# One transfer over 128 partitions in place of two over 64 for each query and key tile of an attention

## The chip, the cores and the metric

The kernel runs on one core of a Trainium2 chip. The metric is the device time of one execution in microseconds, the median of several runs. TensorE (PE) multiplies matrices; VectorE (DVE), ScalarE (ACT) and GpSimd (POOL) work on elements; SyncE (SP) issues most of the transfers between the chip's memory (DRAM) and the on-chip memory (SBUF), which has 128 partitions. ACT and POOL issue some transfers too. 16 DMA engines carry them out.

## The reference

One layer of a decoder trunk over 1024 tokens of width 1024, in float32. Its parts: an input norm and one combined projection; attention over eight heads of 64; an RWKV-7 time mixing; an output projection with a norm and a residual; and a feed-forward block of width 4096. The change touches the attention alone:

```python
h = _rms_norm(x, norm_mix_pre[i])
z = h @ (w_in_first if i == 0 else w_in_rest[i - 1])
q = z[..., 0:D_ATTN]
k = z[..., D_ATTN:2 * D_ATTN]
v = z[..., 2 * D_ATTN:3 * D_ATTN]
...
s = jnp.einsum('bdhnqc,bdhnkc->bdhnqk', qblk, kb) * (1.0 / math.sqrt(Dh))
s = jnp.where(valid, s, -jnp.inf)
p = jnp.exp(s - m[..., None])
acc = jnp.einsum('bdhnqk,bdhnkc->bdhnqc', p, vb)
```

Three branches with different windows and strides are computed and combined by their denominators; the kernel does all three at once, by adding a mask (the "strip") that holds minus the logarithm of how many branches admit a pair of query and key.

## The kernel before

A float32 product is split in the kernel: each operand is a high part, rounded to a shorter type (fp32r), and a low part, the rest. The projection writes the high and the low part of q and k to a DRAM buffer `qk_d` (eight blocks of 128 rows, two parts, 1024 columns; a block holds a pair of heads, 64 rows for each). The high parts are written by ACT's queue (L724), the low ones by POOL's (L725).

The attention goes over four pairs of heads. For a pair p, `at_load` (L881) makes six tiles of 128 partitions by 1024, three for each of its two heads. `qs` has the high part of the head's queries in partitions 0 to 63 and the low part in 64 to 127. `kh` has the high part of the head's keys in both halves, `kl` the low part in both. So a product of `qs` with `kh`, and one with `kl` added to it, give the full scores over a contraction of 128. Each half of each tile is one transfer (L889), issued by SP: 12 for a pair, 48 in all, each 64 rows of 4 KB. The strip is loaded after the first head of pair 0.

The tiles lie in two sets; pairs 0 and 2 use one, pairs 1 and 3 the other, so a load of pair 2 or 3 waits until TensorE is done with the tiles of two pairs before. The set of pairs 1 and 3 lies in memory that comes free when the projection ends, in the course of pair 0.

64 steps, numbered m, go over the pairs, the groups of 128 queries (in the order 0, 4, 1, 5, 2, 6, 3, 7) and the two heads. A step computes the scores (`at_s`, tile `pS`, product by TensorE, mask and row minimum by DVE, exponential by ACT) two steps ahead of the transposes (`at_t`, tile `pT`) and the product with the values (`at_v`, tile `po`). Within pair 0 the second and the third step are exchanged: its first head has two groups before the second head has one. TensorE's order is that of the program text (a manual schedule) and TensorE goes through it strictly; the rest of the last projection (`z_av`) and later the first products of the output projection (`pm`) stand between the steps. The orders of the other engines are made by a scheduler from priorities; each engine then goes through its own strictly too. So does SP: an issue that waits holds back all issues behind it.

`at_load(0)` comes ahead of the steps, `at_load(1)` at m = 8, `at_load(2)` at m = 17 and `at_load(3)` at m = 33. Among SP's issues between them are the values of a pair (`vT`, L896), the output projection's weights (`wo`, L977), inputs for the residual (`xr`, L1047), results of the time mixing (`mr`, L1017) and the attention's output (`a_d`, L966).

The transfers of SP and ACT report their landing on eight counters taken in turn (DMAHW0 to DMAHW7 in the rows below), those of POOL on others (DMASW). A transfer waits until the one before it on its own counter has landed, hence the eighth before it in the program.

Of the kernel before, what the change touches and what calls it, by code (L numbers as in the profile page):

```python
# [10 lines left out]
F32 = mybir.dt.float32  # L11
# [8 lines left out]
P = 128  # L20
S = 1024
# [21 lines left out]
def hybrid_kernel(tc, x, par, cst, strip, win, wup_lora, gup, gnwb, grow, wout, wup, wdown, out, dbg=None):  # L43
    nc = tc.nc
# [21 lines left out]
    with (  # L66
# [60 lines left out]
        qk_d = dp.tile([8, 2, P, S], F32, name="qk_d")  # L127
# [252 lines left out]
        own = (slice(0, 64), slice(64, 128))  # L380
# [452 lines left out]
        st, HVs, VUs, Ys, Ns, N2, VZ, KR, IN, ZP = {}, {}, {}, {}, {}, {}, {}, {}, {}, {}  # L833
# [47 lines left out]
        def at_load(p):  # L881

            T = {(nm, h): aset[p % 2][h].tile([P, S], F32R, name=f"{nm}{p}_{h}", tag=f"{nm}{h}", bufs=1) for h in (1, 0) for nm in ("qs", "kh", "kl")}
            at[p] = QS, KH, KL = [[T[nm, h] for h in range(2)] for nm in ("qs", "kh", "kl")]
            for h in range(2):
                hs_ = slice(64 * h, 64 * h + 64)
                for L, q, js in ((QS, p, (0, 1)), (KH, 4 + p, (0, 0)), (KL, 4 + p, (1, 1))):
                    for d in range(2):
                        nc.sync.dma_start(L[h][own[d]].bitcast(F32), qk_d[q, js[d], hs_, :])  # L889
                if (p, h) == (0, 0):  # L890
                    nc.sync.dma_start(stripT, strip)

# [250 lines left out]
        with hi_pri():  # L1143
            at_load(0)
            at_raw(0)
            at_s(*step(0))
            at_s(*step(1))
        for m in range(64):
            p, h = m // 16, m % 2
            i = m % 16 // 2  # L1150
            with hi_pri():
                if m + 2 < 64:
                    at_s(*step(m + 2))
                at_t(*step(m))
                if h == 1 and i % 2 == 0 and m > 1:
                    at_v(*((p, i - 2) if i else (p - 1, 6)))
                if h == 1 and i == 0:
                    at_vt(p)
                    if p < 3:
                        at_raw(p + 1)  # L1160
                if m == 17 or m == 33:
                    at_load(p + 1)
            if m < RST:
                next(rest, None)
            if m == RST:
                for _ in rest:
                    pass
                open_mix()
                with hi_pri():
                    at_load(1)  # L1170
# [253 lines left out]
        with tc.tile_pool(name="ffd", bufs=1) as fp:  # L1424
            gpF = fp.tile([P, D], F32, name="gpF")
            E1, E2, E3 = ([fp.tile([P, 512], F32, name=f"E{k}_{q}") for q in range(4)] for k in (1, 2, 3))
            st = fp.tile([P, 8, 8], F32, name="stF")
# [202 lines left out]
```

## Time and profile before

| what | value |
|---|---|
| median of 3 runs | 1301.14 us (1300.73 to 1302.78) |
| the profiled execution | 1298.4 us |
| its span, first to last instruction | 1296.6 us |
| memory traffic | 241.08 MB, mean 186 GB/s |
| mean granted TensorE clock | 0.997 |

A row of the lines view gives line, engine, operation, written and read tiles, and count. A row of a timeline gives the start and length in us; in square brackets stand the idle time of the engine before the row and what ended it. "SPq" is SP's issuing of transfers. A row of the list of issues ends in the size of one transfer and the median us from issue to landing. A window row gives the busy time of PE, its weight loads, DVE, ACT and POOL with counts, and then the granted clock of PE, the mean busy share of the 16 DMA engines, and GB/s.

### The profile page before, as it was taken

How to read it: one execution, taken by the hardware profiler on the slowest of the kernel's cores; microseconds unless marked ns; L12 is line 12 of the kernel's file. 1: busy time of each engine (PE TensorE's matmuls, PEld its weight loads, DVE VectorE, ACT ScalarE, POOL GpSimd, SP SyncE). 2: the span in 40 equal slices, each digit the busy share in tenths (PEclk: the TensorE clock that was granted, in tenths of full speed). 3: DMA queues.
4: the chain of work that ended last, by engine and by line, in shares of the span. 5: the costliest groups of instructions: out<-in, count | busy, mean ns of one | idle time of the engine just before them, and what ended most of it. 6: DMA issues, size and time to landing. Idle time of an engine off the chain costs nothing.

```text
span 1296.6 us, 23887 instructions
## 1 busy us (share of the span) xinstructions
PE 1257.5 (97%) x9488; PEld 1035.1 (80%) x9488; DVE 902.8 (70%) x1647; ACT 623.7 (48%) x1052; POOL 43.2 (3%) x61
## 2 busy tenths in 40 slices
PE   6999999999999899999999999999999999999997
PEld 5778888877777678888887888888888888888886
DVE  7877679443868567567879976676666866446884
ACT  8653433233554387666656443444443544443442
POOL 0000000000000000000000000000000002000221
PEclk9999999999999999999999999999999999999999
DMA  6456767976795787314424644444567984556642
GB/s 243 144 191 162 206 159 198 276 219 217 210 264 167 234 238 196 99 56 139 149 96 141 218 142 160 163 146 144 173 210 240 380 296 139 178 189 198 193 160 105
DMA packets 168255, 241.08 MB, mean 186 GB/s; under 512 B 56688, under 2 KB 93808, under 8 KB 168144
## 3 DMA queue, kind: packets, MB, share of 16 engines
q1 hardware_dynamic: 158640, 213.86, 52.8%
q10 hardware_dynamic: 8064, 20.98, 4.8%
q0 software_dynamic: 1440, 4.72, 1.0%
q8 instruction: 75, 1.23, 0.4%
q14 instruction: 36, 0.29, 0.1%
HBM read 162.16 MB, written 77.09 MB: 185 GB/s over the span
## 4 chain that ended last, share of the span: by engine, by line
PE 80%; DVE 7%; DMA 6%; ACT 4%; issue 2%; SPq 1%; ACTq 0%; DVEq 0%
PE dX L49 12%; PE X L49 12%; PE pm L49 7%; PE dZ L49 7%; PE Z L49 6%; PE z_v L49 3%; PE dY L49 3%; PE z_aq L49 3%; PE Y L49 3%; PE z_r L49 3%; PE z_ak L49 2%; PE z_k L49 2%; PE pS L49 2%; PE z_av L49 2%; PE po L49 2%; PE pT L939 2%
## 5 line engine op out<-in xcount | busy, mean ns | idle before, releaser
L49 PE MATMUL dX<-wow,wou 128*128 128x512 f32 x768 | 175.1, 389 | 0.3 <-DVE wow L1247 0.3
L49 PEld LDWEIGHTS dX<-wow,wou 128*128 128x128 f32 x768 | 144.0, 188 | 30.7 <-DVE wow L1247 0.9
L49 PE MATMUL dZ<-wow,wou 128*128 128x512 f32 x384 | 87.4, 389 | 0.0
L49 PEld LDWEIGHTS dZ<-wow,wou 128*128 128x128 f32 x384 | 72.1, 188 | 15.0
L1247 DVE TENSOR_TENSOR wou<-ur,wou 128x1024 fp32r<-128x1024 f32 x56 | 71.2, 1273 | 6.5 <-ACT wou L1246 6.4
L1246 ACT ACTIVATE wow<-wd 128x1024 fp32r<-128x1024 f32 x32 | 33.8, 1060 | 70.6 <-PE dX L49 24.5
L1246 ACT ACTIVATE wou<-ur 128x1024 fp32r<-128x1024 f32 x56 | 58.5, 1048 | 15.6 <-DMA ur<-u_d 8.3
L1247 DVE TENSOR_TENSOR wow<-TK,wow 128x1024 fp32r<-128x1024 f32 x24 | 30.6, 1274 | 50.0 <-ACT wow L1246 50.0
L1247 DVE TENSOR_TENSOR wow<-wd,wow 128x1024 fp32r<-128x1024 f32 x32 | 39.5, 1236 | 29.5 <-ACT wow L1246 29.3
L927 DVE CUSTOM_DVE_ANT_0 S<-pS,stripT 128x512 f32<-128x512 f32 (+3 forms) x64 | 37.7, 589 | 26.3 <-PE pS L49 23.6
L1344 ACT ACTIVATE r<-u 128x512 f32<-128x512 f32 x48 | 30.1, 626 | 53.5 <-DVE u L1342 53.5
L1246 ACT ACTIVATE wow<-TK 128x1024 fp32r<-128x1024 f32 x24 | 25.4, 1059 | 63.0 <-PE dX L49 32.5
L929 ACT ACTIVATE S<-S,mn 128x128 f32<-128x128 f32 (+7 forms) x64 | 49.3, 771 | 11.1 <-DVE mn L927 10.8
L49 PE MATMUL pm<-WO,mxr 128*128 128x512 f32 x192 | 49.1, 400 | 0.8 <-DVE mxr L1012 0.8
L1552 POOL TENSOR_TENSOR E<-E,gpF 128x512 f32<-128x512 f32 x12 | 22.4, 1881 | 781.5 <-DMA xf<-x_d 621.3
L939 PE MATMUL pT<-cst,S 128*128 128x128 f32 x288 | 44.0, 278 | 4.0 <-ACT PT L941 1.7
L49 PE MATMUL z_av<-hT,wh_av 128*128 128x512 f32 x128 | 46.0, 411 | 1.9 <-DVE evl_ak L723 1.9
L49 PE MATMUL pm<-WO,mxa 128*128 128x512 f32 x192 | 46.1, 395 | 0.2 <-ACT mxa L1011 0.2
L49 PE MATMUL Z<-HB,wo 128*128 128x512 f32 x192 | 46.1, 389 | 0.0
L49 PE MATMUL z_aq<-hT,wh_aq 128*128 128x512 f32 x128 | 44.2, 404 | 0.0
L49 PE MATMUL dY<-wow,wou 128*128 128x512 f32 x192 | 43.7, 389 | 0.0
L49 PE MATMUL z_ak<-hT,wh_ak 128*128 128x512 f32 x128 | 43.7, 402 | 0.0
(396 smaller groups left out, 3066.5 us busy)
## 6 DMA issues: line engine op xcount, KB each, us to landing
ur<-u_d SPq DMA_DIRECT2D x56, 512.0 KB, 4.4
u_d<-S SPq DMA_DIRECT2D x64, 256.0 KB, 2.1
wd<-in_wdown_dram SPq DMA_DIRECT2D x32, 512.0 KB, 4.4
u_d<-u SPq DMA_DIRECT2D x48, 256.0 KB, 2.3
TK<-in_wdown_dram SPq DMA_DIRECT2D x24, 512.0 KB, 6.2
wr_upa<-in_wup_dram SPq DMA_DIRECT2D x16, 512.0 KB, 3.5
wr_upb<-in_wup_dram SPq DMA_DIRECT2D x16, 512.0 KB, 4.1
x<-in_x_dram SPq DMA_DIRECT2D x8, 512.0 KB, 7.1
```

The lines of the kernel that those rows point to most:

```text
L49: return PE.matmul(o, lhsT, rhs, start=start, stop=stop, skip_group_check=True)
L927: V.tensor_tensor_reduce(Sx[:, lo:hi], pS[:, :hi - lo], stripT[:, so:so + hi - lo], 1.0, 3e38 if k == 0 else mn[:, 0:1], OP.add, OP.min, a ...
L929: A.activation(Sx[:, :w], Sx[:, :w], AF.Exp, scale=-1.0, bias=mn[:, nbk - 1:nbk], accum_out=at[p, "den"][:, i, h:h + 1])
L939: PE.transpose(pt[:, j], Sx[:, (4 * k + j) * P:(4 * k + j + 1) * P], ident)
L1246: A.activation(w[:, 0, 0:n], raw, AF.Copy)
L1247: low = E.tensor_tensor(w[:, 1, 0:n], raw, w[:, 0, 0:n].bitcast(F32), OP.subtract)
L1344: A.activation(r, src, AF.Relu)
L1552: G.tensor_tensor(e, e, gn[n], OP.mult)
```

## The change

```diff
-                for L, q, js in ((QS, p, (0, 1)), (KH, 4 + p, (0, 0)), (KL, 4 + p, (1, 1))):
-                    for d in range(2):
-                        nc.sync.dma_start(L[h][own[d]].bitcast(F32), qk_d[q, js[d], hs_, :])
+                for L, q, j, st in ((QS, p, 0, P * S), (KH, 4 + p, 0, 0), (KL, 4 + p, 1, 0)):
+                    v = qk_d[q, j, hs_, :]
+                    nc.sync.dma_start(L[h].bitcast(F32), bass.AP(tensor=v.tensor, offset=v.offset, ap=[[st, 2], [S, 64], [1, S]]))
```

A tile is now filled by one transfer. Its source is an access pattern written by hand, a list of steps and counts from the outermost to the innermost. Before, both sides of a transfer were 64 rows of 1024 elements: [[1024, 64], [1, 1024]]. Now the destination is [[1024, 128], [1, 1024]], and the source [[131072, 2], [1024, 64], [1, 1024]] for `qs` (the step from the high part to the low part) and [[0, 2], [1024, 64], [1, 1024]] for `kh` and `kl` (the same 64 rows twice). The program as built carries these patterns unchanged.

SP's order at the load of pair 0, before (`qs_0` is the tile of head 0, `qs_1` of head 1, and `x2` stands for two equal rows):

```order
L889 DMA qs_0_5309<-qk_d 64x1024 x2
L889 DMA kh_0_5310<-qk_d 64x1024 x2
L889 DMA kl_0_5311<-qk_d 64x1024 x2
L891 DMA stripT<-in_strip_dram 128x1024
L889 DMA qs_1_5306<-qk_d 64x1024 x2
L889 DMA kh_1_5307<-qk_d 64x1024 x2
L889 DMA kl_1_5308<-qk_d 64x1024 x2
L896 DMA vT_5325<-zs_d 128x1024
```

and with the change:

```order
L889 DMA qs_0_5309<-qk_d 128x1x1024
L889 DMA kh_0_5310<-qk_d 128x1x1024
L889 DMA kl_0_5311<-qk_d 128x1x1024
L891 DMA stripT<-in_strip_dram 128x1024
L889 DMA qs_1_5306<-qk_d 128x1x1024
L889 DMA kh_1_5307<-qk_d 128x1x1024
L889 DMA kl_1_5308<-qk_d 128x1x1024
L896 DMA vT_5319<-zs_d 128x1024
```

The order is the same, with one issue where two stood.

SP's order from the values of pair 1 over the load of pair 1, before, with what each issue waits for (PE_49 and the like are progress counters of engines):

```order
L896 DMA vT_5395<-zs_d 128x1024 [waits DMAHW6_49,DMAHW3_49,PE_49]
L977 DMA wo_6970<-in_wout_dram 128x1024 [waits DMAHW7_49,DMAHW4_49,DVE_49]
L889 DMA qs_0_5565<-qk_d 64x1024 [waits DMAHW5_49,PE_49]
L889 DMA qs_0_5565<-qk_d 64x1024 [waits DMASW4_49]
L889 DMA kh_0_5566<-qk_d 64x1024 [waits DMAHW0_49]
L889 DMA kh_0_5566<-qk_d 64x1024 [waits DMAHW1_49]
L889 DMA kl_0_5567<-qk_d 64x1024 [waits DMAHW2_49,DMASW7_49,DMASW6_49]
L889 DMA kl_0_5567<-qk_d 64x1024 [waits DMAHW3_49]
L889 DMA qs_1_5562<-qk_d 64x1024 [waits DMAHW4_49]
```

and with the change, up to the first issue of pair 2's load:

```order
L896 DMA vT_5389<-zs_d 128x1024 [waits DMAHW6_49,PE_49]
L889 DMA qs_0_5559<-qk_d 128x1x1024 [waits DMAHW7_49,DMASW4_49,PE_49]
L889 DMA kh_0_5560<-qk_d 128x1x1024 [waits DMAHW1_49]
L889 DMA kl_0_5561<-qk_d 128x1x1024 [waits DMAHW2_49,DMASW7_49,DMASW6_49]
L889 DMA qs_1_5556<-qk_d 128x1x1024 [waits DMAHW3_49]
L889 DMA kh_1_5557<-qk_d 128x1x1024 [waits DMAHW4_49]
L889 DMA kl_1_5558<-qk_d 128x1x1024 [waits DMAHW5_49]
L977 DMA wo_7017<-in_wout_dram 128x1024 [waits DMAHW6_49,DVE_49]
L1047 DMA xr_7462<-in_x_dram 128x1024 [waits DMAHW7_49,DVE_49]
L1047 DMA xr_7535<-in_x_dram 128x1024 [waits DMAHW0_49,DVE_49]
L889 DMA kh_0_5884<-qk_d 128x1x1024 [waits DMAHW1_49,PE_49]
```

The load of pair 1 still follows the `vT` of pair 1 and still waits for PE. Three `wo` and `xr` issues now stand between the loads of pairs 1 and 2; one `wo` issue moved ahead of `vT`. Where before two issues made up a tile, the counters are passed at half the pace, so a wait on a counter reaches back over more tiles.

SP's order at the load of pair 3, before:

```order
L977 DMA wo_7041<-in_wout_dram 128x1024 [waits DMAHW1_49,Activation_49]
L1047 DMA xr_7486<-in_x_dram 128x1024 [waits DMAHW2_49,Activation_49]
L1047 DMA xr_7559<-in_x_dram 128x1024 [waits DMAHW3_49,Activation_49]
L889 DMA qs_0_6384<-qk_d 64x1024 [waits DMAHW4_49,PE_49]
L889 DMA qs_0_6384<-qk_d 64x1024 [waits DMAHW5_49,DMASW6_49,DMASW4_49]
L889 DMA kh_0_6385<-qk_d 64x1024 [waits DMAHW6_49]
L889 DMA kh_0_6385<-qk_d 64x1024 [waits DMAHW7_49]
L889 DMA kl_0_6386<-qk_d 64x1024 [waits DMAHW0_49,DMASW7_49,DMASW1_49]
```

and with the change:

```order
L1047 DMA xr_7634<-in_x_dram 128x1024 [waits DMAHW7_49,DVE_49]
L966 DMA a_d<-ao_0_5820 128x4x128 [waits DMAHW0_49,DVE_49]
L966 DMA a_d<-ao_1_5859 128x4x128 [waits DMAHW1_49,DVE_49]
L896 DMA vT_5878<-zs_d 128x1024 [waits DMAHW2_49,PE_49]
L889 DMA kh_0_6367<-qk_d 128x1x1024 [waits DMAHW3_49,PE_49]
L889 DMA qs_0_6366<-qk_d 128x1x1024 [waits DMASW6_49,DMAHW4_49,DMASW4_49,PE_49]
L889 DMA kl_0_6368<-qk_d 128x1x1024 [waits DMAHW5_49,DMASW7_49,DMASW1_49]
L889 DMA qs_1_6363<-qk_d 128x1x1024 [waits DMAHW6_49,PE_49]
L889 DMA kh_1_6364<-qk_d 128x1x1024 [waits DMAHW7_49]
L889 DMA kl_1_6365<-qk_d 128x1x1024 [waits DMAHW0_49]
```

The issues of `xr` moved ahead, and the two writes of `a_d`, which stood among the tiles' transfers, now stand with the `vT` of the next pair ahead of the load.

Elsewhere the splits of the `wo` weights on ACT and DVE (L983 to L989) move by a few rows. PE's and POOL's orders are unchanged.

## The prediction

> **What bounds the kernel now.** I read the page's first parts, then its chain, then the windows around the loads that the change touches.
>
> ```profile
> span 1296.6 us, 23887 instructions
> PE 1257.5 (97%) x9488; PEld 1035.1 (80%) x9488; DVE 902.8 (70%) x1647; ACT 623.7 (48%) x1052; POOL 43.2 (3%) x61
> PE 80%; DVE 7%; DMA 6%; ACT 4%; issue 2%; SPq 1%; ACTq 0%; DVEq 0%
> ```
>
> PE is busy 97% of the span and its instructions stand in an order fixed by the program, so the time grows by whatever PE is made to wait, and it can shrink by hardly more than the waits that are there. The rows of PE's timeline at which the first head groups of the four pairs begin (a 128x128 form of pS is a first group; the second such row of a pair is its second head) show where PE needs each load. In pair 0 the row at 450.47 is head 0, the one at 452.75 is head 1. For the later pairs the row of the second head alone is quoted.
>
> ```profile
> 447.66 0.50 PE L49 MATMUL z_av<-hT,wh_av 128*128 128x512 f32 x1 [1.94 <-DVE evl_ak L723]
> 450.47 0.31 PE L49 MATMUL pS<-kh,qs 128*128 128x128 f32 x1
> 452.75 0.33 PE L49 MATMUL pS<-kh,qs 128*128 128x128 f32 x1 [0.47 <-DVE mn L927]
> 483.50 0.31 PE L49 MATMUL pS<-kh,qs 128*128 128x128 f32 x1
> 512.92 0.31 PE L49 MATMUL pS<-kh,qs 128*128 128x128 f32 x1
> 548.63 0.22 PE L49 MATMUL pS<-kh,qs 128*128 128x128 f32 x1
> ```
>
> The waits here name DVE, not a load: all loads land ahead of their use, by SP's own times:
>
> ```profile
> 429.21 1.10 SPq L889 DMA_DIRECT2D qs<-qk_d  x2
> 463.00 1.09 SPq L889 DMA_DIRECT2D qs<-qk_d  x2
> 478.23 1.08 SPq L889 DMA_DIRECT2D qs<-qk_d  x2
> 507.56 1.09 SPq L889 DMA_DIRECT2D qs<-qk_d  x2
> qs<-qk_d SPq DMA_DIRECT2D x16, 256.0 KB, 5.2
> kl<-qk_d SPq DMA_DIRECT2D x16, 256.0 KB, 6.7
> ```
>
> The four loads begin 20 to 41 us ahead of the second head of their pair, and one transfer lands in 5.2 to 6.7 us. A pair takes about 30 us of PE (512.92 less 483.50 is 29.4), which is the cover that a load has.
>
> **The change part by part.** It halves the 48 issues of line 889 to 24; the bytes stay: 24 times 512 KB. SP's issuing is not the limit (1.1 us for two issues, above), so this alone is worth nothing. What counts is how a transfer is shared out among the 16 DMA engines. The page's count of the ACT queue tells how it is now:
>
> ```profile
> q1 hardware_dynamic: 158640, 213.86, 52.8%
> q10 hardware_dynamic: 8064, 20.98, 4.8%
> wr_k<-in_win_dram ACTq DMA_DIRECT2D x4, 512.0 KB, 3.5
> ...
> zs_d<-ev_av ACTq DMA_DIRECT2D x8, 256.0 KB, 4.2
> ```
>
> These are the first and last of ten groups of ACT's issues, 56 transfers in all, each of 128 rows; 8064 / 56 is 144, so each has 16 packets beside its rows: one for each of 16 shares. A transfer is cut, and the cut must fall at the same place on both sides. In all transfers of the program before, the first step of either pattern counts 32, 64, 128 or 512, multiples of 16. The new source pattern begins with a step of two (the two halves, or the same half twice), and its halves do not join to one longer step; cut along its first step it gives **two shares**. I take this value: each of the 24 transfers runs on two engines, 64 rows of 4 KB (262,144 bytes) on each. No row of before shows such a transfer; the other end, 16 shares, is the first rival.
>
> The Trainium skill states the rule outright (DMA: Bandwidth & Descriptors, section "Why a DMA increments its semaphore by 16 and not by 1"): the number of engines is the largest up to 16 that divides the size of the slowest dimension larger than one on both sides, which here is 2, and such a transfer goes to the lowest-numbered engines, so all 24 would share the same two. The trace agrees as far as it reaches (16 closing packets where both sides are multiples of 16). By that rule the sum is the one below; were the sharing free of the pattern, it would be the first rival's.
>
> The speed of one engine, from the windows:
>
> ```profile
> 429.00:452.00 23.00, 21.06 (x93) 16.96 (x87) 10.62 (x29) 5.54 (x10) 1.62 (x3) 0.94 0.93 274
> 547.00:590.00 43.00, 43.00 (x578) 37.59 (x577) 26.65 (x72) 28.23 (x61) 0.00 (x0) 1.00 0.21 62
> 1020.00:1035.00 15.00, 15.00 (x68) 12.43 (x67) 12.99 (x12) 8.26 (x10) 0.00 (x0) 1.00 1.05 411
> ```
>
> The last three columns are PE's granted clock, the share of the 16 engines, and GB/s. In the last row an engine moves 411 / (1.05 x 16) = 24.5 GB/s; in the first, where sixteen crowd into 64 partitions, 274 / (0.93 x 16) = 18.4. Two engines alone do not crowd each other, so I take 24.5: 262,144 bytes in 10.7 us, a pair's six transfers in **64.2 us** on both engines; 18.4 would make it 14.2 us a transfer. The 64.2 us stand against a cover of 30, so the load is now the bound.
>
> I follow T, the time at which the second head of a pair has landed; PE can't pass the second head's first product before it, and the first head of that pair is all that it gets done.
>
> T0: the load starts at 429.2; 64.2 of its own; the mask (512 KB over 16 engines, 32 KB on each of the two) 1.3; other traffic: 274 GB/s x 23 us is 6.3 MB, less 4.2 of this load, the mask and vT, leaves 2.1 MB, a sixteenth on each engine, 5.4 us; and a landing delay. For that an unhurried row:
>
> ```profile
> u_d<-S SPq DMA_DIRECT2D x64, 256.0 KB, 2.1
> ```
>
> 16 KB on each engine take 0.7 of the 2.1, leaving 1.4. T0 = 429.2 + 64.2 + 1.3 + 5.4 + 1.4 = 501.5, against 452.75 before: 49 us late already.
>
> T1: load 1 stands on SP behind the vT of pair 1, which waits for PE to have transposed pair 0's, and itself waits for PE; both come after the second head's first product. In before load 1 was issued 463.00 - 452.75 = 10.25 us after that product. So it starts at 511.8 and, behind an idle queue, T1 = 511.8 + 64.2 + 1.4 = 577.4. PE's clock also dips after a wait: 0.94 granted over 23 us in the row of 429 to 452, whose longest wait is the 1.94 us, is 1.4 us lost; I add it here, 578.8.
>
> T2: load 2 waits for PE to finish with pair 0's tiles (478.23 - 452.75 = 25.5 us after T0, at 527), while load 1 is still moving until 577. It stands behind in the queue, and the two engines never go idle: T2 = 578.8 + 64.2 + 4.0 for the wo and two xr loads ahead of it (1.3 each) = 647.0. T3 likewise: load 3 can be issued some 26 us after T1 (605), before load 2 is through: 647.0 + 64.2 + 3.9 (an xr, a vT, two writes of ao) = 715.1, and 1.4 for the clock makes 716.5. The second head of pair 3 started at 548.63 before, and PE is full from there on (43.00 of 43.00 us in the row of 547 to 590), so nothing of it is caught up: **+168 us**.
>
> What else moves costs nothing: one wo load goes behind mr and an ACT/DVE pair of wo splits stands a few rows earlier; both engines idle while PE waits. An issue on ACT that waits for the landing eight transfers earlier (the stores of z_av among the loads) now waits longer, and what is queued behind it on ACT too, but the last such landing, the second head's kh of pair 0, comes 10.7 us ahead of T0. Were PE's wait gone, this would be the next one.
>
> The sum against the profiled execution: 1298.4 + 168 = 1466. The runs' median, 1301.14, lies 2.7 above that execution, so the forecast is **1469**.
>
> **The rivals.** First, the sharing stays sixteenfold whatever the pattern. The loads then land sooner and write all partitions at once. What could be won is shown by the chain and by who waited for the kh tiles:
>
> ```profile
> 431.00 6.31 DMA kh<-qk_d
> 437.33 7.72 DMA kh<-qk_d
>   ACT evh_ak L722: 4.4, 1
> ```
>
> The first load held ACT for 4.4 us, DVE's evl_ak behind it, and PE for 1.94 us (row at 447.66). So between 1.9 and 4.4 us would go, to 1297 to 1299; or, if z_av is then held by DVE anyway, none, 1301. This is the side on which the kernel isn't slower; it decides if the count of shares doesn't hang on the source. The Trainium skill has a rule for it too (the same page, section "Rules for kernel authors"): two transfers to disjoint halves of the partitions share the same 16 engines, so one transfer over 128 is to be used. The 16 closing packets agree with the sixteen engines; that the single transfer keeps them is what no row here shows.
>
> Second, two engines, but at the crowded 18.4 GB/s: 24 transfers by 3.5 us more, +84: 1553. Against it: the crowding shows where sixteen engines write into half of the partitions, and two can't make it.
>
> Third, two engines, but only the first load is exposed, the others being hidden because they are issued early: T0's 49 us alone, 1350. Against it: 64 us against 30 us a pair, and load 1 can't be issued before T0.
>
> **How the numbers follow.** The forecast has 0.70, the crowded rate 0.15, sixteen shares 0.11, the hidden loads 0.04. The reason for 0.85 on two engines bound throughout is that a cut along both patterns leaves no other number; what speaks against is only that no row shows it. Low end: without the other traffic and small loads on the two engines (5.4 + 4.0 + 3.9), the clock's 2.8 and the 10.25 of load 1, 1469 - 26 = 1443, so 1440; high end: the crowded 1553. The range 1440 to 1553 holds the forecast and most of the second rival. A measurement of this kernel tells about 0.2% (2.6 us) from no change. Slower by more: 0.70 + 0.15 + 0.04 = 0.89; of the 0.11, 0.04 faster and 0.07 the same.
>
> **What would show it.** In the changed profile's queue list, q1's packets: 48 transfers of 64 rows and 16 closers (3840) go; with two shares 24 x 130 = 3120 come, 157,920 in all; with sixteen 24 x 144 = 3456, 158,256. Landing of qs, kh and kl: above 10 us at least and up to some 60 where they queue, against medians of 5.2 to 6.7 us. From 430 to 715 the DMA share falls to 0.1 to 0.25. PE's chain should name these loads, with one long wait before the second head of each pair, ending near 501, 577, 647 and 715; the steps are right if the differences are 76, 70 and 68. Wrong it is if q1 has 158,256 packets, or if the differences are near 30.

## The result, and the profile after

| | before | with the change |
|---|---|---|
| median of 5 runs each | 1302.64 us (1300.73 to 1307.24) | 1465.53 us (1461.89 to 1466.92) |
| the profiled execution | 1298.4 us | 1461.89 us |
| ratio | | 1.1242 (95% interval 1.1213 to 1.1271) |

The kernel became 12% slower; forecast were 1469 us. Against the before measured beside it, the change cost 162.9 us, where 168 were forecast. The page of the changed kernel, its lines on the span, PE, PE's clock in 40 slices, SP's queue and the chain:

```profile
span 1459.8 us, 23852 instructions
PE 1266.2 (87%) x9488; PEld 1041.2 (71%) x9488; DVE 903.0 (62%) x1647; ACT 624.6 (43%) x1052; POOL 43.1 (3%) x61
PEclk9999999999997585968799999999999999999999
q1 hardware_dynamic: 157920, 213.86, 45.4%
PE 72%; DMA 10%; SPq 8%; DVE 6%; ACT 3%; issue 1%; DVEq 0%; ACTq 0%
```

SP's queue has 157,920 packets with the same bytes: the number forecast for two shares. PE does the same work; from slice 12 to 19 (counted from 0) its granted clock falls to between 0.5 and 0.8, but for slice 16. In the chain that ended last, transfers and SP's issuing together have 18% in place of 7%. A window in which PE does nothing shows what is left of the traffic (last columns: PE's clock, the share of the 16 engines, GB/s):

```profile
536.00:566.00 30.00, 0.00 (x0) 0.00 (x0) 0.00 (x0) 0.00 (x0) 0.00 (x0) 0.50 0.13 53
```

0.13 of 16 engines is 2.1 engines, at 53 GB/s. With the transfers of 16 shares that run among the loads, the mean share is 0.32 from 429 to 505 us and 0.20 from 515.7 to 710.4; the prediction had 0.1 to 0.25. The largest rows of the view of who waited for whom, on PE from 425 to 760 us (total us, times, longest):

```profile
PE pT L939 <- ACT PT L941: 53.4, 6, 51.8
PE pS L49 <- DMA kh<-qk_d: 38.7, 3, 17.8
PE pS L49 <- DVE mn L927: 37.5, 1, 37.5
PE pS L49 <- DMA kl<-qk_d: 29.7, 3, 10.3
```

They come to 159.3 us, where the same view of before from 425 to 600 has no row above 1.9. The span grew by 163.2: PE's idle time by 154.5 (193.6 less 39.1, span less busy time), since these waits are new and some small ones went, and its busy time by 8.7 (1266.2 less 1257.5). So nearly all the lost time is PE waiting in the attention. That the 8.7 is work done at the lower clock after each wait fits the clock's row, but is not tried by itself. The rows of PE's timeline that stand for the prediction's steps:

```profile
455.52 0.44 PE L49 MATMUL pS<-kh,qs 128*128 128x128 f32 x1 [6.21 <-DMA kh<-qk_d]
465.76 0.47 PE L49 MATMUL pS<-kl,qs 128*128 128x128 f32 x1 [9.80 <-DMA kl<-qk_d]
504.67 0.48 PE L49 MATMUL pS<-kh,qs 128*128 128x128 f32 x1 [37.48 <-DVE mn L927]
505.28 0.47 PE L49 MATMUL pS<-kh,qs 128*128 128x128 f32 x1
584.21 1.12 PE L939 MATMUL pT<-cst,S 128*128 128x128 f32 x4 [51.82 <-ACT PT L941]
591.13 0.31 PE L49 MATMUL pS<-kh,qs 128*128 128x128 f32 x1
635.31 0.44 PE L49 MATMUL pS<-kh,qs 128*128 128x128 f32 x1 [14.65 <-DMA kh<-qk_d]
645.40 0.48 PE L49 MATMUL pS<-kl,qs 128*128 128x128 f32 x1 [9.65 <-DMA kl<-qk_d]
699.71 0.45 PE L49 MATMUL pS<-kh,qs 128*128 128x128 f32 x1 [17.80 <-DMA kh<-qk_d]
710.43 0.47 PE L49 MATMUL pS<-kl,qs 128*128 128x128 f32 x1 [10.28 <-DMA kl<-qk_d]
```

The first two rows are head 0 of pair 0: PE took kh and kl as they landed, 10.24 us apart. 505.28 is the first product of pair 0's second head, 591.13 that of pair 1's; 584.21 is a transpose that still belongs to pair 0. In pairs 2 and 3 the second head begins at 635.31 and 699.71 with kh, and goes on at 645.40 and 710.43 with kl, its last tile; all four wait for the load itself. The two long waits that name DVE and ACT have a wo load at their start, by ACT's timeline (a wo split is the cut of an output weight into its high and low part):

```profile
502.05 0.63 ACT L988 ACTIVATE WO<-wo 128x512 fp32r<-128x512 f32 x1 [44.55 <-DMA wo<-in_wout_dram]
582.34 1.33 ACT L983 ACTIVATE WO<-wo,par 128x512 fp32r<-128x512 f32 x2 [51.89 <-DMA wo<-in_wout_dram]
```

SP's timeline shows the speed:

```profile
515.74 0.50 SPq L889 DMA_DIRECT2D qs<-qk_d  x1
516.29 0.51 SPq L889 DMA_DIRECT2D kh<-qk_d  x1
516.90 1.47 SPq L889 DMA_DIRECT2D kl<-qk_d  x1
518.42 18.45 SPq L889 DMA_DIRECT2D qs<-qk_d  x1
536.92 9.74 SPq L889 DMA_DIRECT2D kh<-qk_d  x1
676.17 9.74 SPq L889 DMA_DIRECT2D kl<-qk_d  x1
```

The first three issues of load 1 pass nearly at once; the fourth is held for 18.45 us, and the fifth takes 9.74, as later ones do. I read this as SP going on by one issue when one transfer has left the queue. A transfer then takes 9.74 us, 26.9 GB/s for each of two engines (262,144 bytes), and the window above agrees (53 GB/s for both). The trace gives no landing times for SP's transfers here, so the forecast on landings is not tried.

### The profile page after: what moved, and what is told of

Read it like the earlier page. It is cut to its first block, busy times and chain, and to the rows that moved or that the text cites. A ratio compares the mean times of both kernels' runs of the same rounds, so it can differ in the third digit from the quotient of the medians.

```text
span 1459.8 us, 23852 instructions
## 1 busy us (share of the span) xinstructions
PE 1266.2 (87%) x9488; PEld 1041.2 (71%) x9488; DVE 903.0 (62%) x1647; ACT 624.6 (43%) x1052; POOL 43.1 (3%) x61
## 3 DMA queue, kind: packets, MB, share of 16 engines
q1 hardware_dynamic: 157920, 213.86, 45.4%
q10 hardware_dynamic: 8064, 20.98, 4.3%
q0 software_dynamic: 1440, 4.72, 0.9%
## 4 chain that ended last, share of the span: by engine, by line
PE 72%; DMA 10%; SPq 8%; DVE 6%; ACT 3%; issue 1%; DVEq 0%; ACTq 0%
PE X L49 11%; PE dX L49 11%; SPq L889 6%; PE dZ L49 6%; PE pm L49 6%; PE Z L49 6%; DMA kl<-qk_d 5%; PE z_v L49 3%; DMA wo<-in_wout_dram 3%; PE z_aq L49 3%; PE dY L49 3%; PE Y L49 2%; PE z_ak L49 2%; PE z_av L49 2%; PE z_r L49 2%; PE z_k L49 2%
## 5 line engine op out<-in xcount | busy, mean ns | idle before, releaser
L49 PE MATMUL pS<-kh,qs 128*128 128x512 f32 (+3 forms) x96 | 38.5, 401 | 76.1 <-DMA kh<-qk_d 38.7
L939 PE MATMUL pT<-cst,S 128*128 128x128 f32 x288 | 46.3, 289 | 54.4 <-ACT PT L941 53.4
L939 PEld LDWEIGHTS pT<-cst,S 128*128 128x128 f32 x288 | 34.5, 147 | 61.9 <-ACT PT L941 58.3
L49 PEld LDWEIGHTS pS<-kh,qs 128*128 128x128 f32 x96 | 19.6, 204 | 82.2 <-issue 39.7
L1246 ACT ACTIVATE wow<-wd 128x1024 fp32r<-128x1024 f32 x32 | 33.8, 1060 | 70.2 <-PE dX L49 24.5
L49 PE MATMUL pS<-kl,qs 128*128 128x512 f32 (+3 forms) x96 | 34.2, 366 | 29.7 <-DMA kl<-qk_d 29.7
L1247 DVE TENSOR_TENSOR wow<-wd,wow 128x1024 fp32r<-128x1024 f32 x32 | 39.5, 1236 | 26.9 <-ACT wow L1246 26.4
L941 ACT ACTIVATE PT<-pT 128x512 f32<-128x512 f32 (+3 forms) x64 | 32.7, 511 | 45.8 <-PE pT L939 45.3
```

The costliest lines, as they stand in the source:

```text
L49: return PE.matmul(o, lhsT, rhs, start=start, stop=stop, skip_group_check=True)
L939: PE.transpose(pt[:, j], Sx[:, (4 * k + j) * P:(4 * k + j + 1) * P], ident)
L941: A.activation(PT[:, 0:nb_], pt[:, 0:nb_], AF.Copy)
L1246: A.activation(w[:, 0, 0:n], raw, AF.Copy)
L1247: low = E.tensor_tensor(w[:, 1, 0:n], raw, w[:, 0, 0:n].bitcast(F32), OP.subtract)
```

## The experiments

**The same transfer, its rows first.** The two outer steps of the source are exchanged; the tile's rows are permuted alike for queries and keys, so the sums are the same. Every engine's order is that of the changed kernel. The end of the changed line alone:

```diff
-ap=[[st, 2], [S, 64], [1, S]]
+ap=[[S, 64], [st, 2], [1, S]]
```

> The changed kernel with the two outer steps of the source exchanged: 64 rows first, the two halves second. Still 24 transfers over 128 partitions of the same bytes from the same places; query and key rows are permuted alike within a tile, so the scores are the same sums. Theory A (the source's first step of two confines a transfer to two engines): the first step now is 64, so each has 16 shares, q1 has 158,256 packets, and the time is that of before or slightly less, 1296 to 1303. Theory B (a transfer of 128 partitions gathered from two places, or with a step of zero, is slow in itself): nothing changes, about 1465 and 157,920 packets.

Measured: 1304.06 us, ratio 1.001 (0.9989 to 1.0031). Its page's line on SP's queue, its window of load 0 (last columns: clock, share, GB/s), its largest wait of PE from 425 to 600, and the split that stands ahead of the first mask step on DVE:

```profile
q1 hardware_dynamic: 158256, 213.86, 51.3%
```

```profile
428.00:446.00 18.00, 17.22 (x94) 13.93 (x90) 7.86 (x22) 3.73 (x7) 1.08 (x2) 1.00 0.92 333
```

```profile
PE pS L49 <- DMA wo<-in_wout_dram: 4.4, 1, 4.4
```

```profile
451.33 0.69 DVE L989 TENSOR_TENSOR WO<-wo,WO 128x512 fp32r<-128x512 f32 x1 [2.27 <-ACT WO L988]
```

158,256 packets, 16 shares, and the whole loss is gone; the time is 1 us above theory A's range, and the same as before's within the interval. The count of shares hangs on the source's first step; neither the 128 partitions nor the step of zero (still there, as the second) costs anything that can be measured. Theory B falls. That the time isn't below before's, though loading is quicker, goes with the last two fences: in the scheduler's new order a wo split stands ahead of the first mask step on DVE (at 453.84), and PE waits 4.4 us for that wo's load.

**The queries alone, the keys alone.** The kernel before, with one kind of tile loaded as the change does. The added lines, for the queries:

```diff
+                    if L is QS:
+                        v = qk_d[q, js[0], hs_, :]
+                        nc.sync.dma_start(L[h].bitcast(F32), bass.AP(tensor=v.tensor, offset=v.offset, ap=[[P * S, 2], [S, 64], [1, S]]))
+                        continue
                     for d in range(2):
```

For the keys the condition is `L is not QS` and the first step 0.

> The kernel before with the query tiles alone loaded as the change does (8 such transfers; the keys in halves). Theory A with two shared engines and a cover of some 29 us for a pair: two such transfers take 20 us of the two engines and the rest of the load 7, so the load nearly hides; only pairs 0 and 1 are late, by 9 and 6 us: 1310 to 1322. Rival C (each such transfer costs its share of the 163 us, 6.8, outright): 8 x 6.8 = 54, 1356. Rival B with the step of zero as the cause: 1301, since the queries have no step of zero.

> The kernel before with the key tiles alone loaded as the change does (16 such transfers; the queries in halves). Theory A: four such transfers take 40 us of the two engines in each pair, some 12 to 20 more than the cover with the rest of the load, and the first load is wholly exposed: late by 26, 48, 65 and 75 us at the four pairs, 1365 to 1390. Rival C: 16 x 6.8 = 109, 1411. Rival B with the step of zero as the cause: near 1411 as well, or more.

Measured: queries alone 1348.72 us, ratio 1.0362 (1.0334 to 1.039); keys alone 1406.24 us, 1.0803 (1.0772 to 1.0833). Both lie above theory A's ranges, nearer to rival C's totals. Rival B with the step of zero falls: the queries have none, and 1301 was its number. The rows of PE's timeline with the queries alone, second head of each pair, and the wait between pairs 1 and 2; then ACT's row behind that wait, and SP's longest wait in the first load:

```profile
468.80 0.45 PE L49 MATMUL pS<-kl,qs 128*128 128x128 f32 x1 [1.25 <-DMA kl<-qk_d]
515.50 0.44 PE L49 MATMUL pS<-kl,qs 128*128 128x128 f32 x1 [1.30 <-DMA kl<-qk_d]
548.98 0.90 PE L943 MATMUL pT<-cst,S 128*128 128x128 f32 x3 [13.47 <-ACT PT L945]
562.09 0.31 PE L49 MATMUL pS<-kh,qs 128*128 128x128 f32 x1
597.84 0.27 PE L49 MATMUL pS<-kl,qs 128*128 128x128 f32 x1
```

```profile
547.83 0.72 ACT L987 ACTIVATE WO<-wo,par 128x512 fp32r<-128x512 f32 x1 [13.27 <-DMA wo<-in_wout_dram]
```

```profile
SPq L893 <- DMA qs<-qk_d: 12.6, 1, 12.6
```

Against before the pairs are late by 16, 32, 49 and 49 us (468.80 less 452.75, and so on). Pair 3's load costs nothing: 597.84 less 562.09 is 35.75, against 548.63 less 512.92, 35.71, before. A price for each transfer outright, rival C, can't give that; but A's sum was too small in three places. The first two loads were longer than I took them to be (16 us late instead of 9, and 16 more instead of 6): in the first, SP issued nothing from 434.94 to 447.55, because the issue of the second head's kh waits for the landing of a slow qs, 12.6 us. And I had given load 1 the cover of a whole pair, 29 us; since it can't be issued earlier, its cover is 483.50 less 463.00, 20.5. And pair 1 lost 13.47 us more by a wait for ACT, which I had not seen: ACT had waited 13.27 us for a wo, which SP issued at 540.68, behind load 2. With the keys alone the loads stay on the path to the end:

```profile
606.18 0.47 PE L49 MATMUL pS<-kl,qs 128*128 128x128 f32 x1 [11.59 <-DMA kl<-qk_d]
657.03 0.47 PE L49 MATMUL pS<-kl,qs 128*128 128x128 f32 x1 [10.60 <-DMA kl<-qk_d]
```

These are the second heads of pairs 2 and 3. Against before the four pairs are late by 40, 79, 93 and 108 us (PE's rows at 492.31 and 562.66, and these two), where theory A had 26, 48, 65 and 75. 7.1 us of each are the later start of load 0 in the profiled execution (436.35 against 429.21), and a wait of 26.70 us for ACT behind a wo load, as with the queries, stands ahead of pair 1's second head; the rest is not taken apart. From pair 2 to pair 3 are 50.85 us, 15 more than before: four transfers of 9.74 are 39.0 and exceed the pair's 35.7 by themselves, and the rest of the load comes on top. So two transfers a pair hide once the queue has caught up, and four don't.

**The wo loads by POOL.** In the changed kernel PE went on at 504.67 behind DVE, and DVE had waited for a wo split:

```profile
502.71 0.69 DVE L989 TENSOR_TENSOR WO<-wo,WO 128x512 fp32r<-128x512 f32 x1 [44.32 <-ACT WO L988]
```

```diff
-            nc.sync.dma_start(raw, wout[k * P:(k + 1) * P, :])
+            nc.gpsimd.dma_start(raw, wout[k * P:(k + 1) * P, :])
```

> The changed kernel with the loads of the output projection's weights (wo) issued by POOL instead of SP, so that they do not queue behind the query and key loads. In the changed kernel PE went on only at 504.67, after DVE and ACT had the wo tile, though the second head had landed at some 499.6; and in pair 1 it waited until 584.21 with ACT behind a wo that landed at 582, where the second head had landed at 581. Theory A (the two engines' queue sets the end, the wo waits only ride on it): the 4 to 5 us at pair 0 are won, since load 1 starts that much sooner, and nothing more: 1457 to 1463. Rival D (the waits for wo are on the path by themselves): 8 us and more at pair 1 besides, below 1453.

Measured: 1466.85 us, ratio 1.126 (1.1217 to 1.1303), which is the number of neither. Load 0 began at 435.59, 6.3 us later than in the changed kernel (429.27), so I repeated it with the wo loads ahead of load 0 left on SP:

```diff
-            nc.sync.dma_start(raw, wout[k * P:(k + 1) * P, :])
+            (nc.sync if 4 <= k < 7 else nc.gpsimd).dma_start(raw, wout[k * P:(k + 1) * P, :])
```

> The changed kernel with the five wo loads that stand behind load 0 on SP (wo 7, 0, 1, 2, 3) issued by POOL; the three ahead of it stay on SP, so that load 0 begins as in the changed kernel. In the run with all wo loads on POOL it began 6.3 us later (435.59 against 429.27), which hid what the wo waits were worth. Theory A: PE goes on at pair 0 when the second head has landed, 499 to 503, instead of 504.67; load 1 begins some 3 us sooner, pair 1's wait of 51.82 us for ACT turns into one for a load, and the end moves by no more than those 3 us: 1459 to 1466. Rival D (the waits for wo are on the path by themselves): 8 us or more: below 1457.

Measured: 1464.01 us, ratio 1.1219 (1.1186 to 1.1253), the changed kernel's time within the intervals. PE's waits, 425 to 760:

```profile
PE pS L49 <- DMA kh<-qk_d: 89.2, 6, 20.6
PE pS L49 <- DMA kl<-qk_d: 65.0, 7, 14.1
PE pT L939 <- ACT PT L941: 1.4, 4, 0.6
```

The waits for ACT (53.4 us) and for DVE's mn (37.5) are gone, those for kh and kl grew from 68.4 to 154.2, and the time is the same. So the waits named ACT and DVE in the changed kernel were the queue's: a wo load behind the key loads, a split behind the wo. Rival D falls; of the 3 us that theory A allowed, 1.5 show between the medians (1465.53 less 1464.01) and 3.0 between the ratios to the before measured beside each (1.1242 and 1.1219), both inside the intervals. In the profiled execution load 0 began 3.3 us later (432.57), which may hold some of it. As the run with the keys alone, where wo stays on SP, began its loads late as well (436.35), I don't put the later start down to POOL.

**Which engines.** The second head's loads, 12 of the 24, are issued by another engine: by POOL, or by ACT (`nc.scalar` in place of `nc.gpsimd`). The start of the changed line alone:

```diff
-                    nc.sync.dma_start(
+                    (nc.gpsimd if h else nc.sync).dma_start(
```

> The changed kernel with the loads of every second head (12 of the 24) issued by POOL, through its own queue, with the same patterns. Theory A (all of SP's two-share transfers go to the same two engines, one behind the other) leaves open which engines POOL's queue takes. If others, or more than two, the six transfers of a pair run as three and three side by side, some 30 us a pair, and the time falls to 1330 to 1390. Rival E (each such transfer is slow whichever engines carry it, one at a time): 1450 or more.

> The changed kernel with the loads of every second head issued by ACT. Theory A with the engines fixed by the pattern and not by the queue: ACT's transfers take the same two engines as SP's, so these still carry 24 transfers of 9.9 us and nothing is won; ACT, which goes through its order strictly, is held besides: 1455 to 1500. Rival F (each issuing queue has engines of its own for such a transfer): 30 us a pair and 1330 to 1390.

Measured: by POOL 1375.63 us, ratio 1.0531 (1.0501 to 1.0561); by ACT 1466.92 us, 1.1238 (1.1185 to 1.1291). The queue lines with ACT as the second issuer, then two issues of SP in that run, and a window in which both queues have such transfers waiting:

```profile
q1 hardware_dynamic: 156360, 207.57, 44.3%
q10 hardware_dynamic: 9624, 27.27, 5.3%
```

```profile
579.47 19.48 SPq L889 DMA_DIRECT2D kl<-qk_d  x1
646.31 18.64 SPq L889 DMA_DIRECT2D kl<-qk_d  x1
```

```profile
585.00:605.00 20.00, 19.04 (x269) 16.73 (x266) 12.44 (x40) 12.75 (x32) 0.00 (x0) 0.94 0.14 55
```

q10 rose from 8064 by 1560, 12 times 130: two shares each here as well. With two queues going, an issue takes 19.48 us, twice 9.74, and the share is 0.14 at 55 GB/s, two engines' worth for both queues together: ACT's transfers run on the same two engines as SP's. Nothing is won, as theory A had it; rival F falls. By POOL:

```profile
q1 hardware_dynamic: 156360, 207.57, 47.2%
q0 software_dynamic: 13920, 11.05, 2.7%
```

```profile
PE z_av L49 <- DVE evl_ak L723: 35.8, 1, 35.8
PE pT L939 <- ACT PT L941: 26.3, 4, 25.0
PE pS L49 <- DMA kl<-qk_d: 11.1, 2, 9.6
```

```profile
483.99 1.15 ACT L988 ACTIVATE WO<-wo 128x512 fp32r<-128x512 f32 x2 [43.43 <-DMA r_d<-Y]
484.66 1.29 DVE L989 TENSOR_TENSOR WO<-wo,WO 128x512 fp32r<-128x512 f32 x2 [42.23 <-ACT WO L988]
```

PE's direct waits for the loads shrink to 11.1 us for kl, in place of the 29.7 and the 38.7 for kh, and the time lies in the range for loads side by side; rival E's 1450 falls. The rest of the loss still comes from such transfers. Half of it is PE's wait for evl_ak (the low part of k, on its way to `qk_d`), and the last two rows follow it: evl_ak stands on DVE (at 485.87) behind two wo splits, these wait for ACT's, and the trace puts ACT's wait down to a store, r_d. POOL issued that store at 442.99, behind its three loads, and it landed 40.9 us later; these loads of POOL's land 24.9 to 39.8 us after issue (medians of qs, kh and kl). The 25.0 us for ACT's PT have a wo load on SP at their start (ACT waits 25.11 us for it). So moving half of the loads to POOL made a second slow queue. How POOL's transfers are shared out isn't told by these lines.

**A version that could beat both.** Rows interleaved, and the five wo loads by POOL.

> The run with the rows interleaved (16 shares), and the five wo loads behind load 0 issued by POOL. With the rows interleaved the 1.9 us wait of before for evl_ak shrank to 1.5, but a new wait of 4.42 us for a wo load came, because the first wo split now stands ahead of the first mask step on DVE. Theory A: the wo loads no longer stand behind load 0, the 4.42 go, and the time is 3 to 5 us below that run, 1296 to 1301, some 0.1 to 0.4% below before. Rival G: POOL's issues come later than SP's, or take longer to land, and the wait stays: 1301 to 1306.

Measured: 1302.31 us, ratio 1.0019 (0.9997 to 1.0041). In place of the 4.4 us for wo PE waits 3.42 us for DVE's mn (row at 456.27 of its timeline), and ACT's row shows the same load at its start:

```profile
454.05 1.15 ACT L988 ACTIVATE WO<-wo 128x512 fp32r<-128x512 f32 x2 [3.16 <-DMA wo<-in_wout_dram]
```

That is rival G: POOL issued this wo at 449.43, once DVE was done with an earlier wo, and it landed 4.6 us later. No version here is measurably faster than the kernel before.

## Why the prediction was right

**Two shares.** The step on which everything hung, that the cut goes along the patterns' first steps, held to the packet: 157,920 by the count, and 158,256 with a first step of 64. The share of the engines agrees, 0.13 with only these transfers running, and 0.14 with SP and ACT issuing both, an issue then taking 19.48 us against 9.74. By the Trainium skill's rule on how many engines a transfer takes (DMA: Bandwidth & Descriptors, section "Why a DMA increments its semaphore by 16 and not by 1"), such a source gives two shares on trn2, and such transfers from SP and from ACT go to the same lowest-numbered engines. The packets and the run with ACT agree; which two engines they are, no view here shows. The Trainium skill's other rule (same page, section "Rules for kernel authors") is to use one transfer over 128 partitions in place of two halves. Here that cost 1.1242 with the two halves as the first step, and with the rows first, 1.001, it brought no loss and no gain that can be measured.

**One engine's speed.** 10.7 us a transfer were taken, 9.74 measured while the queue was full. 24.5 GB/s came from sixteen engines at once; two moved 26.9 each. The crowded 18.4 of the second rival is out.

**T0.** 501.5 forecast, PE resumed at 504.67. It was reached by another way: not the second head's load, but DVE, held 44.32 us by a wo split, let PE go. I had written that the wo splits which stand a few rows earlier cost nothing because both engines idle meanwhile; a split that stands ahead of a mask step takes its load's landing along, and that load stood behind load 0. It was a wrong sentence with little in it here (the run with five wo loads by POOL). In the interleaved version such a split costs PE 4.4 us; what the time would be without any such wait no run shows, since with the loads moved to POOL 3.42 us of it stayed.

**T1.** Load 1 began at 515.74, 10.46 us after the second head's first product at 505.28 (10.25 taken). PE went on at 584.21, but with pair 0's work that the wo split had held; the second head began at 591.13, 12 us later than the 578.8 forecast. So the first head of pair 1 was not "all that it gets done": PE got less done. This was not lost for good, because load 2 was in the queue by then.

**T2 and T3.** 645.40 and 710.43 against 647.0 and 715.1. The steps from one second head to the next were forecast as 76, 70 and 68 us; PE's rows give 85.9, 54.3 and 65.0. The first two are off because of pair 1's late start, the third by the faster transfers; the sum, 205.2 against 214, is what the queue sets. And there was not one long wait a pair: PE waits for each tile as it lands. That the two engines never go idle held: in windows of 3 us from 521 to 710 the traffic never falls below 48 GB/s. From load 1's issue to T3 are 194.7 us, where 203.3 were forecast: 18 transfers at 0.96 less take 17.3 off, and 8.7 were added that I did not have (perhaps the start of the queue and the small transfers; not taken apart).

**After T3.** 1459.8 less 710.43 is 749.4, before 1296.6 less 548.63 was 748.0: nothing was caught up, and 1.4 us more were needed. The clock explains them, as taken: in the first window behind T3 PE is full, but at a granted clock of 0.74 over 5.57 us, which is an estimated 1.4 us less of work; after it PE runs at full clock again:

```profile
710.43:716.00 5.57, 5.57 (x28) 4.64 (x28) 2.50 (x8) 2.87 (x7) 0.00 (x0) 0.74 0.04 14
716.00:760.00 44.00, 43.90 (x569) 37.75 (x569) 25.35 (x69) 27.91 (x58) 0.00 (x0) 1.00 0.26 85
```

The forecast is 3.5 us too high, and the difference to before 5 too high (168 against 162.9): faster transfers, less the terms that were missing. That the errors leave so little is in part luck.

**The rivals.** Sixteen shares: out by the packets; in the interleaved run, which has them, the second of its two prices held, no gain that can be measured (the 1.94 us wait for evl_ak fell only to 1.48). Hidden loads behind the first: out for six transfers a pair, and the true case, in part, for two.

## What to carry to other kernels

Look at a transfer's first step on both sides before counting its bytes: 24 transfers fewer in number cost 163 us because their source began with a step of two, and the same transfers with 64 first cost nothing. Packets per transfer (rows plus one closer for each share) tell it from the page, for the queues of SP and ACT. Where a queue is held, the waits are named after whoever stands last in the chain; moving that one away moved 86 us of waits to the loads and won no time that can be measured.

## What had not been expected

SP itself stops: with some three such transfers ahead, an issue takes 9.74 us and up to 18.45, and all of SP's later issues, whatever their shares, wait with it.

POOL's queue cut the same transfers differently: q0 grew from 1440 packets by 12,480, 1040 for each of the 12 transfers, and by 6.33 MB, some 500 bytes a packet, where SP's had 130 packets. 1040 is 1024 packets of 512 bytes and 16 more, which by the count used above would be sixteen shares; but from 472 to 482 us, with POOL's queue not yet through (r_d lands at 483.9), the share is 0.13, two engines' worth. So for POOL's queue the packets alone don't tell the shares.

Sixteen engines that load 128 partitions moved 333 / (0.92 x 16) = 22.6 GB/s each in the interleaved run's load 0, where the halves of 64 partitions before moved 18.4 in a like stretch. Why, no run here tries.
